# Gate and up products of two FFNs as seven block products instead of eight, on one Trainium2 core

## The chip, the cores and the metric

The kernel runs on one NeuronCore of a Trainium2 chip. The metric is the device time of one launch in microseconds. Three runs of the kernel before gave 1391.13 us as their median, between 1390.26 and 1394.65 us. Engines are named as in the profile: PE multiplies matrices, PEld is its weight load, DVE and ACT work elementwise, POOL works elementwise and issues transfers whose descriptors it writes itself, SP issues the other transfers.

## The reference

Two layers, each a token mixer (RWKV-7 in layer 0, a gated spatial unit in layer 1) followed by a dense SwiGLU FFN, all between two RMS norms with a residual. Only the FFN and the norm ahead of it matter here (512 tokens, 1024 features, 2816 hidden features, all float32):

```
h = x * rsqrt(mean(x*x) + 1e-6) * gain          # per token
h = (silu(h @ w_gate) * (h @ w_up)) @ w_down    # 1024 -> 2816 -> 1024
x = x + rmsnorm(h) * gain_post
```

## The kernel before

Every float32 matrix product is made of three products of a shorter float type: each operand is split into a high part (an ACT copy that rounds) and a low part (a DVE subtraction of the rounded from the raw), and `mm3` (line 153) adds high·high, high·low and low·high into one PSUM bank. `weight` (line 134) loads a 512 KB weight tile through SP's queue, casts it on ACT (line 131 or 147) and subtracts on DVE (line 132) or, for the first tiles of a stage, on POOL (line 148). Two buffers of raw weights and four of split ones let these run ahead of PE.

The order is RWKV, FFN 0, spatial unit, FFN 1. Each ends in `out_proj` (line 229), which multiplies by the output matrix in two column halves and keeps the last weight units for the end, so that the tokens finish in four blocks of 128: `post0` and `post1` make the norm behind the product and the new residual `x`, and the next stage's norm follows two blocks behind (`norm.step`). `Norm.step` (line 48) transposes the raw `x` on PE, multiplies by the gain and splits into `hT`; the factor 1/rms of each token is left out and comes in behind the products: `Norm.row` (line 70) spreads the four columns of factors over all partitions as a row `yb`.

In `ffn` (line 302) a loop goes over 22 tiles `j` of 128 hidden features. For each, the gate and the up weight tile (128 columns, all 1024 rows as 8 blocks `kt`) are multiplied by `hT`: 2 x 8 x 3 = 48 matmuls of 512 tokens; the first two tiles do it in two halves of 256 tokens, because the later tokens' norm comes later. Then line 330 (DVE) multiplies the gate result by `yb`, line 331 (ACT) applies silu, line 332 (DVE) multiplies by the up result, line 333 (POOL) by `yb`, and the product is split at once for the down product.

The program is written in one order; a planner with a cost model decides at compile time the order of each engine's instructions and gives out the buffers. PSUM has eight banks, given to stages by the tables `BANKS_RWKV` and `BANKS` (lines 28 to 30). SBUF has 17 slots of tag "s" and, in the stages behind RWKV, 13 of tag "x", each of 4 KB per partition.

Of the kernel before, what the change touches and what calls it, by code (L numbers as in the profile page):

```python
# [7 lines left out]
F32 = mybir.dt.float32  # L8
# [5 lines left out]
P = 128  # L14
# [15 lines left out]
BANKS = dict(pa=(3, 4, 0, 7), pb=(1, 2, 5, 6), h0=(1, 2, 5, 6), h1=(3, 4, 0, 7), tr=(1, 2, 5, 6))  # L30
# [9 lines left out]
class Norm:  # L40
# [29 lines left out]
    def row(self):  # L70

        k, nc = self.k, self.k.nc
        t = k.sm.tile([P, D], F32, name="hn", tag="hn", bufs=2)
        yb, dg = t[:, 0:T], t[:, T:2 * T]
        pt = k.bank("tr", "yb")
        for tt in range(TT):
            nc.gpsimd.tensor_scalar(dg[:, tt * P:(tt + 1) * P], k.ident, self.y[tt][:, 0:1], None, op0=ALU.mult)
        nc.tensor.matmul(pt, k.ones, dg, start=True, stop=True)
        nc.scalar.copy(yb, pt)
        return yb  # L80


class Trunk:
# [69 lines left out]
    def mm3(self, out, lhs, rhs, start, stop):  # L153

        mm = self.nc.tensor.matmul
        mm(out, lhs[0], rhs[0], start=start, stop=False)  # L156
        mm(out, lhs[0], rhs[1], start=False, stop=False)  # L157
        mm(out, lhs[1], rhs[0], start=False, stop=stop)  # L158
# [64 lines left out]

    def start_x(self, xts, norm):
        for tt in range(TT):
            norm.step(tt, xts[tt])
        norm.finish()
# [74 lines left out]
    def ffn(self, li, xts, norm, store=None, nxt=None):  # L302
        nc = self.nc
        gains = self.i["norm_gains"]
        wg = self.i["ffn_w_gate"][li].rearrange("(kt p) n -> p kt n", p=P)
        wu = self.i["ffn_w_up"][li].rearrange("(kt p) n -> p kt n", p=P)
        wd = self.i["ffn_w_down"][li].rearrange("(u j p) n -> u p j n", p=P, j=2)
        acts = []
        hT, yb = norm.hT, None
        def products(j, ws, acc, a, b):  # L310
            for w, ps in zip(ws, acc):
                for kt in range(KT):
                    self.mm3(ps[:, a:b], (w[0][:, kt, :], w[1][:, kt, :]), (hT[kt][:, 0, a:b], hT[kt][:, 1, a:b]),
                             kt == 0, kt == KT - 1)

        first = []
        for j in range(NJ):
            if not first:
                for n in range(j, j + 1):
                    cols = slice(n * P, (n + 1) * P)  # L320
                    first.append(([self.weight(w[:, :, cols], pool=n < 2) for w in (wg, wu)],
                                  [self.pa("gu") for _ in range(2)]))
                halves = ((0, 256), (256, 512)) if j < 2 else ((0, 512),)
                for a, b in halves:
                    for ws, acc in first:
                        products(j, ws, acc, a, b)
            pp = first.pop(0)[1]
            sg = self.fp.tile([P, T], F32, name="sg", tag="sg", bufs=1)
            yb = norm.row() if yb is None else yb
            nc.vector.tensor_tensor(sg, pp[0], yb, op=ALU.mult)  # L330
            nc.scalar.activation(sg, sg, AF.Silu)
            nc.vector.tensor_tensor(sg, sg, pp[1], op=ALU.mult)  # L332
            nc.gpsimd.tensor_tensor(sg, sg, yb, op=ALU.mult)  # L333
            act = self.slot([P, 2, T], F32R, "act", "x" if j < XSLOTS else "s")
            self.split(act[:, 0, :], act[:, 1, :], sg)
            acts.append(act)
        self.out_proj(lambda k: (acts[k][:, 0, :], acts[k][:, 1, :]), lambda u: wd[u], NJ, gains[li, 3], xts, store, norm=nxt)
# [33 lines left out]
    def rwkv(self, x0, nxt):  # L371
# [3 lines left out]
        with ExitStack() as ctx:  # L375
# [619 lines left out]
            norm = self.prenorm("g02") if nxt else None  # L995
# [4 lines left out]
    def sgu(self, xts, norm, nxt):  # L1000
# [64 lines left out]
        for m in range(8):  # L1065
# [3 lines left out]
            t = self.fp.tile([P, T], F32, name="sg", tag="sg", bufs=1)  # L1069
# [10 lines left out]
def build(tc, ins, out, only=None):  # L1080
    with ExitStack() as ctx:
# [6 lines left out]
        norm = None  # L1088
        if only in (None, "rwkv"):
            xts, norm = k.rwkv(xts, only is None)  # L1090
        if only != "rwkv":
            k.tags = BANKS
            k.fp = ctx.enter_context(tc.tile_pool(name="fp", bufs=1))
            k.wx = ctx.enter_context(tc.tile_pool(name="wx", bufs=2))
            k.sx = ctx.enter_context(tc.tile_pool(name="sx", bufs=1))

        def begin(col, norm):
            if norm is None:
                norm = k.prenorm(col)
                k.start_x(xts, norm)  # L1100
            return norm

        if only in (None, "ffn"):
            nxt = k.prenorm("g10") if only is None else None
            k.ffn(0, xts, begin("g02", norm), out[0] if only else None, nxt)
            norm = nxt
        if only in (None, "sgu"):
            nxt = k.prenorm("g12") if only is None else None
            k.sgu(xts, begin("g10", norm), nxt)
            norm = nxt  # L1110
        if only is None:
            k.ffn(1, xts, norm, out[0])
        elif only != "ffn":
            for t in range(TT):
                nc.sync.dma_start(out=out[0, t * P:(t + 1) * P, :], in_=xts[t])
# [26 lines left out]
```

## Time and profile before

| | |
|---|---|
| median of three runs | 1391.13 us |
| span of the profiled execution | 1389.8 us |
| PE busy in it | 1326.0 us (95%) |
| DVE / ACT / POOL busy | 753.5 / 604.0 / 224.9 us |
| FFN 0, first gate matmul to first down matmul | 483.3 to 735.9 us |
| FFN 1, first gate matmul to last | 1012.0 to 1260.4 us |
| bytes moved in the whole span | 139.90 MB, mean 101 GB/s |

The profile gives for the profiled execution only its span, so sums are made against 1389.8 us; the median of the runs lies 1.3 us above. Busy time of PE is modelled: a matmul of 512 columns is shown with 0.39 us, though the next starts 0.23 us after it. So the distance between starts is what is read in the following, not the duration. A span's busy share is a mean over stages; the FFN's gate and up stage is read by itself.

### The profile page before, as it was taken

To read this page: it belongs to the slowest core of one execution; us is meant where nothing else is said; L and a number is where in the kernel's file an instruction comes from. 1 tells how busy PE (TensorE), PEld (TensorE's weight loads), DVE (VectorE), ACT (ScalarE), POOL (GpSimd) and SP (SyncE) were. 2 spreads that over 40 slices of the span, in tenths; PEclk is the share of its full clock that TensorE was granted. 3 is DMA by queue.
4 is the path that set the end of the run, shared out by engine and by line. 5 is a ranking of instruction groups with operands and counts; after the bars stand their busy time and mean duration, and the time that the engine had idled before them with its cause. 6 is when DMAs were issued, how large, how long until landed. Compare 5 with 4: busy or idle time off the path is not lost.

```text
span 1389.8 us, 21566 instructions
## 1 busy us (share of the span) xinstructions
PE 1326.0 (95%) x8512; PEld 1080.3 (78%) x8512; DVE 753.5 (54%) x1309; ACT 604.0 (43%) x1100; POOL 224.9 (16%) x347
## 2 busy tenths in 40 slices
PE   5989999988899899999999999999999999999998
PEld 3657789877776698888888887878888888888886
DVE  7875666577746565455542325575565544453223
ACT  7865785667343453232322224542463322232121
POOL 1000283675000121111110002010221111110000
PEclk9999999999799999999999999999999999999999
DMA  5135594323114143333333232342323333322331
GB/s 154 44 97 145 139 223 153 101 75 94 67 46 148 48 120 94 103 92 91 91 91 106 92 106 91 106 137 76 91 83 98 93 91 98 100 91 91 92 105 61
DMA packets 216100, 139.90 MB, mean 101 GB/s; under 512 B 66704, under 2 KB 192192, under 8 KB 216000
## 3 DMA queue, kind: packets, MB, share of 16 engines
q1 hardware_dynamic: 214704, 133.81, 33.1%
q0 software_dynamic: 1296, 4.72, 1.0%
q8 instruction: 67, 1.10, 0.3%
q14 instruction: 33, 0.27, 0.1%
HBM read 124.35 MB, written 14.16 MB: 100 GB/s over the span
## 4 chain that ended last, share of the span: by engine, by line
PE 83%; DVE 6%; ACT 4%; DMA 3%; issue 2%; POOL 1%; SPq 0%; DVEq 0%; ACTq 0%; POOLq 0%
PE gu L156 12%; PE gu L158 12%; PE gu L157 12%; PE acc L156 9%; PE acc L157 8%; PE acc L158 8%; PE proj L157 2%; PE proj L156 2%; PE proj L158 2%; PE gh L821 2%; PE lora L494 1%; PE lm L706 1%; PE u L157 1%; PE u L158 1%; PE u L156 1%
## 5 line engine op out<-in xcount | busy, mean ns | idle before, releaser
L131 ACT CAST whi<-wraw 128x1024 fp32r<-128x1024 f32 x177 | 185.8, 1049 | 487.4 <-PE gu L157 252.6
L132 DVE TENSOR_TENSOR wlo<-wraw,whi 128x1024 fp32r<-128x1024 f32 x177 | 263.1, 1486 | 226.0 <-ACT whi L131 218.5
L157 PE MATMUL gu<-hT,whi 128*128 128x512 f32 (+1 forms) x768 | 288.6, 377 | 1.4 <-DVE hT L59 1.4
L156 PE MATMUL gu<-hT,whi 128*128 128x512 f32 (+1 forms) x768 | 289.1, 379 | 0.3 <-ACT hT L57 0.3
L158 PE MATMUL gu<-hT,wlo 128*128 128x512 f32 (+1 forms) x768 | 288.6, 377 | 0.0
L157 PEld LDWEIGHTS gu<-hT,whi 128*128 128x128 f32 x768 | 145.1, 189 | 30.5 <-DVE hT L59 1.6
L156 PEld LDWEIGHTS gu<-hT,whi 128*128 128x128 f32 x768 | 145.0, 190 | 29.4 <-ACT hT L57 0.5
L158 PEld LDWEIGHTS gu<-hT,wlo 128*128 128x128 f32 x768 | 144.9, 189 | 28.6
L157 PE MATMUL acc<-wlo,act 128*128 128x512 f32 x416 | 163.8, 394 | 0.0
L156 PE MATMUL acc<-whi,act 128*128 128x512 f32 x416 | 163.7, 395 | 0.0
L158 PE MATMUL acc<-whi,act 128*128 128x512 f32 x416 | 160.4, 394 | 0.0
L333 POOL TENSOR_TENSOR sg<-sg,hn 128x512 f32<-128x512 f32 x44 | 58.0, 1318 | 417.4 <-DVE sg L332 417.4
L332 DVE TENSOR_TENSOR sg<-sg,gu 128x512 f32<-128x512 f32 x44 | 30.3, 688 | 142.4 <-PE gu L158 140.2
L158 PEld LDWEIGHTS acc<-whi,act 128*128 128x128 f32 x416 | 78.1, 188 | 18.2
L156 PEld LDWEIGHTS acc<-whi,act 128*128 128x128 f32 x416 | 78.2, 188 | 18.0
L157 PEld LDWEIGHTS acc<-wlo,act 128*128 128x128 f32 x416 | 78.1, 188 | 18.0
L330 DVE TENSOR_TENSOR sg<-gu,hn 128x512 f32<-128x512 f32 x44 | 30.4, 691 | 67.3 <-PE gu L158 67.1
L131 ACT CAST act<-sg 128x512 fp32r<-128x512 f32 x52 | 32.4, 622 | 73.4 <-POOL sg L333 59.2
L156 PE MATMUL proj<-xsp,whi 128*128 128x512 f32 x128 | 52.2, 413 | 3.5 <-ACT xsp L131 3.1
L157 PE MATMUL proj<-xsp,whi 128*128 128x512 f32 x128 | 52.2, 409 | 2.2 <-DVE xsp L132 2.2
L148 POOL TENSOR_TENSOR wlo<-wraw,whi 128x1024 fp32r<-128x1024 f32 x12 | 29.0, 2424 | 145.4 <-ACT whi L147 145.4
L158 PE MATMUL proj<-xsp,wlo 128*128 128x512 f32 x128 | 52.1, 408 | 0.1
(321 smaller groups left out, 2187.5 us busy)
## 6 DMA issues: line engine op xcount, KB each, us to landing
wraw<-in_ffn_w_gate_dram SPq DMA_DIRECT2D x44, 512.0 KB
wraw<-in_ffn_w_up_dram SPq DMA_DIRECT2D x44, 512.0 KB, 3.8
wraw<-in_ffn_w_down_dram SPq DMA_DIRECT2D x44, 512.0 KB, 3.6
wraw<-in_rwkv_w_rkv_dram SPq DMA_DIRECT2D x24, 512.0 KB, 4.5
wraw<-in_sgu_w_in_dram SPq DMA_DIRECT2D x16, 512.0 KB, 3.7
x<-in_x_dram SPq DMA_DIRECT2D x8, 512.0 KB, 5.9
ST<-sb SPq DMA_DIRECT2D x8, 512.0 KB, 6.3
MV<-sa SPq DMA_DIRECT2D x32, 128.0 KB, 3.2
```

Of the source, the lines that this page charges most:

```text
L131: self.nc.scalar.copy(hi, src)
L132: self.nc.vector.tensor_tensor(lo, src, hi.bitcast(F32), op=ALU.subtract)
L148: nc.gpsimd.tensor_tensor(lo, raw, hi.bitcast(F32), op=ALU.subtract)
L156: mm(out, lhs[0], rhs[0], start=start, stop=False)
L157: mm(out, lhs[0], rhs[1], start=False, stop=False)
L158: mm(out, lhs[1], rhs[0], start=False, stop=stop)
L330: nc.vector.tensor_tensor(sg, pp[0], yb, op=ALU.mult)
L332: nc.vector.tensor_tensor(sg, sg, pp[1], op=ALU.mult)
L333: nc.gpsimd.tensor_tensor(sg, sg, yb, op=ALU.mult)
L494: mm(acc, w1m[j][:, kt].rearrange("p j n -> p (j n)"), src(kt), start=j == 0 and kt == 0, stop=j == 1 and kt == KT - 1)
L706: mm(lm[:, cc * P:(cc + 1) * P], st[:, cc].rearrange("p n t -> p (n t)"), mv[:, cc, :, hd, :], start=True, stop=True)
L821: mm(gh[:, cc * P:(cc + 1) * P], mt[rows, cc, :], bx[rows, 0:2, cc, :], start=True, stop=True)
```

## The change

The gate and up products of each FFN are done for two hidden tiles (a pair `n`, 11 pairs) at a time as 2 x 2 blocks: two halves of the contraction, two hidden tiles, two halves of the tokens. A plain block product takes eight products of a block; here it takes seven, of sums of blocks. A product is now 2 (gate, up) x 4 (kt) x 3 = 24 matmuls of 256 tokens with 24 weight blocks; its gate and up results share one PSUM bank, 256 columns each.

- The token side: `Mixed` takes the place of `Norm` ahead of the FFNs. It finishes the norm before the transpose (squares, root, one DVE multiplication of the whole 128 x 1024 block), so `yb` and line 333 are gone. Blocks 1 and 2 (the first 256 tokens) are split when the second token block is there; `combine` makes and splits the five others from sums once all four are there.
- The weight side: per pair three single blocks are loaded by SP (`quad`), and each of the seven operands is cast on ACT and subtracted on DVE. Four operands are sums. Two of them (`dsum`) are made by transfers on POOL's queue: one that writes, and one with `accum_op` that adds to what is there, each as two transfers of 256 KB for gate and up; the two others are DVE additions onto the first sum.
- The results: three banks R, Q, Z gather products, with partial sums copied by ACT from Q, R and Z; Q starts as a copy of R into PSUM, and matmuls go on adding to it, for which one matmul in each Q bank is issued first.
- The order in a pair is p5, p6, p7, p3, p4 for the first two pairs, whose p1 and p2 are done ahead of `combine`, and p1, p5, p6, p2, p7, p3, p4 afterwards.
- The split of the hidden activation for the down product moves into `out_proj`, where it is done when first used. POOL no longer subtracts the first weight tiles of an FFN.

```diff
-BANKS = dict(pa=(3, 4, 0, 7), pb=(1, 2, 5, 6), h0=(1, 2, 5, 6), h1=(3, 4, 0, 7), tr=(1, 2, 5, 6))
+BANKS_F0 = dict(tr=(1, 2), R=(3, 4), Q=(5, 0), Z=(7, 6), h0=(1, 2, 4, 0), h1=(3, 5, 7, 6))
+BANKS_SGU = dict(tr=(1, 2), pa=(3, 5, 7, 6), h0=(1, 2, 4, 0), h1=(3, 5, 7, 6))
+BANKS_F1 = dict(tr=(1, 2), R=(4, 0), Q=(3, 5), Z=(7, 6), h0=(1, 2, 0, 5), h1=(4, 3, 7, 6))
...
+class Mixed:
...
+    def split(self, name, src, tag):
+        k = self.k
+        hi, lo = (k.slot([P, 4, 256], F32R, "bc", tag) for _ in range(2))
+        k.split(hi, lo, src)
+        self.b[name] = (hi, lo)
+
+    def step(self, tt, xt):
...
+        t = k.sm.tile([P, D], F32, name="hn", tag="hn", bufs=2)
+        s = [k.sumsq(xt[:, c:c + 512], t[:, c:c + 512]) for c in (0, 512)]
+        y = k.rsqrt1(s[1], k.part(s[0], 1.0 / D, RMS_EPS), 1.0 / D)
+        v.scalar_tensor_tensor(t, xt, y[:, 0:1], self.gain, op0=ALU.mult, op1=ALU.mult)
+        for j in range(2):
+            pt = k.bank("tr", "ptr")
+            for n in range(4):
+                kt = 4 * j + n
+                nc.tensor.transpose(pt[:, n * P:(n + 1) * P], t[:, kt * P:(kt + 1) * P], k.ident)
+            nc.scalar.copy(self.raw[j, l][:, :, (tt % 2) * P:(tt % 2 + 1) * P], pt.rearrange("p (n t) -> p n t", n=4))
+        if tt == 1:
+            self.split(1, self.raw[0, 0], "s")
+            self.split(2, self.raw[1, 0], "s")
...
+    def combine(self):
+        k, v = self.k, self.k.nc.vector
+        b11, b21, b12, b22 = (self.raw[p] for p in ((0, 0), (1, 0), (0, 1), (1, 1)))
+        t1, t2 = (k.slot([P, 4, 256], F32, "tsum", "x") for _ in range(2))
+        v.tensor_tensor(t1, b11, b12, op=ALU.subtract)
+        self.split(5, t1, "x")
+        v.tensor_tensor(b12, b22, b12, op=ALU.subtract)
+        v.scalar_tensor_tensor(t2, b12, -1.0, b11, op0=ALU.mult, op1=ALU.subtract)
+        self.split(6, t2, "x")
+        self.split(7, b12, "x")
+        self.split(3, b22, "x")
+        v.scalar_tensor_tensor(b21, t2, -1.0, b21, op0=ALU.mult, op1=ALU.subtract)
+        self.split(4, b21, "x")
...
     def ffn(self, li, xts, norm, store=None, nxt=None):
...
+        def quad(n, j, f):
+            pool, tag = ((self.wp, "wraw"), (self.f0p, "f0"), (self.gp, "gain"))[loads[0] % 3]
...
+            for m, w in enumerate(wgu):
+                nc.sync.dma_start(out=t[:, m], in_=w[:, 4 * j:4 * j + 4, (2 * n + f) * P:(2 * n + f + 1) * P])
+            return t
+
+        def product(ps, name, src, start=False):
+            self.nw += 1
+            wp = self.wx if self.nw % 2 else self.wp
+            hi, lo = (wp.tile([P, 2, 4, P], F32R, name=t, tag=t, bufs=2) for t in ("whi", "wlo"))
+            self.split(hi, lo, src)
+            bh, bl = b[name]
+            for m in range(2):
+                for kt in range(4):
+                    self.mm3(ps[:, 256 * m:256 * m + 256], (hi[:, m, kt], lo[:, m, kt]), (bh[:, kt], bl[:, kt]),
+                             start and m == 0 and kt == 0, m == 1 and kt == 3, True)
+
+        def dsum(n, *parts):
+            s = self.slot([P, 2, 4, P], F32, "wsum", "x")
+            for op, (j, f) in zip((ALU.bypass, ALU.add), parts):
+                for m, w in enumerate(wgu):
+                    nc.gpsimd.dma_start(out=s[:, m], in_=w[:, 4 * j:4 * j + 4, (2 * n + f) * P:(2 * n + f + 1) * P], accum_op=op)
+            return s
+
+        def p1(n):
...
+            product(o["R"], 1, o["a11"], True)
...
+            a.copy(o["Q"], o["R"])
...
+        def p5(n):
...
+            o["a22"] = quad(n, 1, 1)
+            o["s"] = dsum(n, (0, 1), (1, 1))
...
+            product(o["Z"], 5, o["s"], True)
...
+            a.copy(o["t"][:, 0], o["Z"])
+
+        def p6(n):
+            o = pairs[n]
+            v.tensor_tensor(o["s"], o["s"], o["a11"], op=ALU.add)
+            product(o["Q"], 6, o["s"])
+            a.copy(o["t"][:, 1], o["Q"])
+
+        def p7(n):
+            o = pairs[n]
+            product(o["Q"], 7, dsum(n, (0, 0), (0, 1)))
...
+            v.scalar_tensor_tensor(o["cc"][:, 1], o["Q"], -1.0, o["t"][:, 0], op0=ALU.mult, op1=ALU.subtract)
+
+        def p3(n):
+            o = pairs[n]
+            v.tensor_tensor(o["s"], o["s"], o["a12"], op=ALU.add)
+            product(o["Z"], 3, o["s"])
+            cc = o["cc"]
+            v.tensor_tensor(cc[:, 0], o["Z"], o["t"][:, 1], op=ALU.add)
+            a.activation(cc[:, :, g], cc[:, :, g], AF.Silu)
+            v.tensor_tensor(o["act"][:, :, u], cc[:, :, g], cc[:, :, u], op=ALU.mult)
+
+        def p4(n):
+            o = pairs[n]
+            product(o["Q"], 4, o["a22"])
+            gate(o["act"][:, 1, g], o["Q"], -1.0)
+
+        for n in range(2):
+            p1(n)
+            p2(n)
+        norm.combine()
+        for n in range(NJ // 2):
+            for p in (p5, p6, p7, p3, p4) if n < 2 else (p1, p5, p6, p2, p7, p3, p4):
+                p(n)
+
+        halves = {}
+
+        def down(k):
+            if k not in halves:
+                t = halves[k] = self.slot([P, 2, T], F32R, "actw", "x" if k < XSLOTS else "s")
+                self.split(t[:, 0], t[:, 1], acts[k // 2][:, k % 2])
+            return halves[k][:, 0], halves[k][:, 1]
```

`p2(n)` loads the fourth kind of single block as p1 does, multiplies it by block 2 into R and applies `gate` (a silu of 256 columns on ACT and a DVE product with the up half).

More of the change, by code (lines that the diff above doesn't have):

```diff
@@ L303, in ffn @@
         nc = self.nc
+        v, a = nc.vector, nc.scalar
         gains = self.i["norm_gains"]
-        wg = self.i["ffn_w_gate"][li].rearrange("(kt p) n -> p kt n", p=P)
-        wu = self.i["ffn_w_up"][li].rearrange("(kt p) n -> p kt n", p=P)
+        wgu = [self.i[n][li].rearrange("(kt p) n -> p kt n", p=P) for n in ("ffn_w_gate", "ffn_w_up")]
         wd = self.i["ffn_w_down"][li].rearrange("(u j p) n -> u p j n", p=P, j=2)
[L308 to L336, printed above, removed]
@@ new lines, in dsum @@
+        def dsum(n, *parts):
[5 more added lines that the diff above has]
+        def p1(n):
+            o = pairs[n] = dict(act=self.slot([P, 2, T], F32, "act"))
+            acts.append(o["act"])
+            o["a11"] = quad(n, 0, 0)
+            o["R"] = self.bank("R", "R")
+            product(o["R"], 1, o["a11"], True)
+            if len(seeded) < 2:
+                q = self.bank("Q", "Q")
+                seeded.append(q)
+                bh = b[1][0]
+                nc.tensor.matmul(q, bh[:, 0, 0:P], bh[:, 0:2].rearrange("p k t -> p (k t)"), start=True, stop=True)
+            o["Q"] = seeded[n % 2]
+            a.copy(o["Q"], o["R"])
@@ new lines, in gate, with p2 @@
+        def gate(dst, src, sign=1.0):
+            sg = self.fp.tile([P, 256], F32, name="sg", tag="sg", bufs=2)
+            a.activation(sg, src[:, g], AF.Silu, scale=sign)
+            if sign == 1.0:
+                v.tensor_tensor(dst, sg, src[:, u], op=ALU.mult)
+            else:
+                v.scalar_tensor_tensor(dst, src[:, u], sign, sg, op0=ALU.mult, op1=ALU.mult)
+        def p2(n):
+            o = pairs[n]
+            o["a12"] = quad(n, 1, 0)
+            product(o["R"], 2, o["a12"])
+            gate(o["act"][:, 0, g], o["R"])
@@ new lines, in p4 @@
+        def p4(n):
+            o = pairs[n]
+            product(o["Q"], 4, o["a22"])
[13 more added lines that the diff above has]
+            return halves[k][:, 0], halves[k][:, 1]
@@ L340, in load_features @@
+        self.out_proj(down, lambda u: wd[u], NJ, gains[li, 3], xts, store, norm=nxt)
     def load_features(self):
```

84 lines of the change are left out of this document (44 added, 40 removed).

## The prediction

> **What bounds the kernel now.** I read the page's totals and chain first.
>
> ```profile
> span 1389.8 us, 21566 instructions
> PE 1326.0 (95%) x8512; PEld 1080.3 (78%) x8512; DVE 753.5 (54%) x1309; ACT 604.0 (43%) x1100; POOL 224.9 (16%) x347
> ...
> PE 83%; DVE 6%; ACT 4%; DMA 3%; issue 2%; POOL 1%; SPq 0%; DVEq 0%; ACTq 0%; POOLq 0%
> ```
>
> PE carries 83% of the chain that ended last. Next I read busy time by stretch for the two gate and up stages (columns: length, then PE, PEld, DVE, ACT, POOL busy with counts, granted clock, DMA share, GB/s).
>
> ```profile
> 484.00:510.00 26.00, 23.94 (x184) 23.25 (x185) 19.42 (x60) 17.41 (x49) 8.62 (x8) 0.93 0.34 98
> 510.00:735.00 225.00, 225.00 (x984) 182.48 (x983) 114.61 (x104) 69.20 (x84) 27.30 (x21) 1.00 0.34 98
> ...
> 1035.00:1260.00 225.00, 225.00 (x980) 182.08 (x980) 113.37 (x104) 68.64 (x83) 27.04 (x21) 1.00 0.33 98
> ```
>
> In both, PE never pauses, at full clock; DVE is half busy, ACT a third, the DMA engines a third. So these stages last as long as their matmuls, and fewer columns streamed means less time, as long as the others keep up. What a matmul costs is the distance of starts. In the timeline, line 332 runs once per hidden tile, at the same place of each; between two 256-column rows there are 18 matmuls.
>
> ```profile
> 602.38 0.69 DVE L332 TENSOR_TENSOR sg<-sg,gu 128x512 f32<-128x512 f32 x1 [3.55 <-PE gu L158]
> ...
> 635.82 0.69 DVE L332 TENSOR_TENSOR sg<-sg,gu 128x512 f32<-128x512 f32 x1 [3.55 <-PE gu L158]
> ```
> ```profile
> 502.38 0.28 PE L156 MATMUL gu<-hT,whi 128*128 128x256 f32 x1
> ...
> 504.52 0.28 PE L156 MATMUL gu<-hT,whi 128*128 128x256 f32 x1
> ```
>
> Three tiles of 48 matmuls take 33.44 us: 0.2322 us per 512 columns. 18 matmuls of 256 take 2.14 us: 0.119 us, or 2.4% more per column. That price already holds a new weight block for every matmul.
>
> **The change: PE.** A pair had 2 x 48 = 96 matmuls of 512: 22.29 us. It gets 7 x 24 = 168 of 256: 19.99 us, 2.30 us less, a product taking 2.86 us. Over 11 pairs that is 25.3 us; the first two tiles were in halves already (96 more of 256 each pair of halves: 192 x 0.119 = 22.85 against 22.29), another 0.6. Two FFNs: 2 x 25.9 = **-51.8 us**. The four matmuls that open the Q banks and the two dropped ones of `yb` cancel to half a microsecond.
>
> **The steady pair on the other engines.** These rows price what it needs (duration; or count, min/median/max in ns).
>
> ```profile
> L132 DVE TENSOR_TENSOR wlo<-wraw,whi x177: 1177/1226/2367, 19.1 to 1361.8; 128x1024 fp32r<-128x1024 f32 x177
> L132 DVE TENSOR_TENSOR act<-sg,act x52: 676/678/693, 516.4 to 1264.0; 128x512 fp32r<-128x512 f32 x52
> ```
> ```profile
> L131 ACT CAST act<-sg 128x512 fp32r<-128x512 f32 x52 | 32.4, 622 | 73.4 <-POOL sg L333 59.2
> ```
> ```profile
> L131 ACT CAST whi<-wraw 128x1024 fp32r<-128x1024 f32 x41 | 43.1, 1052 | 122.0 <-PE gu L157 119.4 <-DMA wraw<-in_ffn_w_up_dram 2.0 <-DMA wraw<-in_ffn_w_gate_dram 0.6
> L331 ACT ACTIVATE sg<-sg 128x512 f32<-128x512 f32 x22 | 13.9, 633 | 4.1 <-DVE sg L330 4.0
> ```
> ```profile
> 465.45 0.42 DVE L930 TENSOR_TENSOR ob<-gate,ob 128x256 f32<-128x256 f32 x1 [1.83 <-PE gate L929]
> 507.94 0.59 ACT L79 COPY hn<-yb 128x512 f32<-128x512 f32 x1
> 603.15 1.30 POOL L333 TENSOR_TENSOR sg<-sg,hn 128x512 f32<-128x512 f32 x1 [9.84 <-DVE sg L332]
> 603.17 2.37 DVE L132 TENSOR_TENSOR wlo<-wraw,whi 128x1024 fp32r<-128x1024 f32 x1
> ```
>
> DVE: seven subtractions and two additions of 1024 at 1.23 = 11.1 us, one combination of 512 from PSUM, one addition, one product (0.69 each) and two gates of 256 (0.42): 14.0 us of 20.0. ACT: seven casts at 1.05, three PSUM copies at 0.59, a silu of 0.63 and two of 256 (bounded by 0.63 each): 11.0 us. Neither binds. POOL's multiplication and DVE's subtraction, which started together (603.15 and 603.17), stretched the latter to 2.37; with line 333 gone that doubling goes, worth nothing now, but it is why 1.23 is the price afterwards.
>
> The waits inside a pair: ACT's copy of R into Q has p5 between it and the next user, the copy of Q after p6 has p2, DVE's read after p7 has p3, each a cover of 2.86 us for 0.6 to 0.7. So nothing, except in the first two pairs, where p2 follows p1 and p7 follows p6 directly; without the cover each costs about 0.9 us (0.59 and a handover). The split of the activations moves into the down stage: 0.62 + 0.68 us each, two per unit of 24 x 0.2322 = 5.57 us beside a weight's 1.05 and 1.23; ACT 2.3 and DVE 2.6 of 5.57, hidden.
>
> **The transfers.** SP issues six of 256 KB per pair instead of four of 512 KB. POOL issues eight, which no row shows in this size or with accumulation; the nearest:
>
> ```profile
> L1008 POOL DMA_DIRECT2D wsr<-in_sgu_ws_dram x1: 988/988/988, 800.2 to 800.2; - x1
> ...
> DMA to landing us min/median/max: 5.6/5.6/5.6
> ```
> ```profile
> L180 POOL DMA_DIRECT2D gain<-in_norm_gains_dram x4: 531/534/758, 408.4 to 979.5; - x4
> ```
>
> `wsr` has 1024 rows of 512 bytes, a gain 128 of 4 KB; 512 rows lie between, some 0.75 us of issue: 6 us per pair. Two halves of a plain `dsum` land within 5.6 us (twice the bytes). Bytes: 2.62 MB plain per pair, at the stage's 98 / 0.34 = 288 GB/s 9.1 us of the DMA engines, and 1.05 MB accumulated, from the same rate (3.6 us) to a third of it (10.9 us; it reads two places and writes one): 12.7 to 20.0 of 20.0 us. I take half the rate, 7.3: 82%, not binding. The chain of one sum is two issues, a landing, two issues, a second landing of X, cast and subtraction: 1.5 + 5.6 + 1.5 + X + 1.05 + 1.23 = 10.9 + X, and its buffer comes free only after the subtraction (of 13 "x" slots ten hold token blocks, three rotate). It is hidden to X = 9.1. I take X = 5.6, hidden, and keep the rest as a rival. Behind a waiting second transfer on POOL stand only the next sum's transfers; behind a cast that waits for them stand ACT's bank copies, and so PE.
>
> The Trainium skill (SBUF — State Buffer, "SBUF: two separate sides") says that a DVE operation in a 2-port mode keeps POOL from writing descriptors until it ends. No run here shows it; if each of the eight issues waited out one subtraction, POOL would need 8 x (0.75 + 1.23) = 15.8 us of 20, an estimate that leaves the sum alone.
>
> **The start of each FFN.** Here the change costs.
>
> ```profile
> 479.65 0.39 PE L158 MATMUL acc<-whi,oT 128*128 128x512 f32 x1
> ...
> 483.31 0.50 PE L156 MATMUL gu<-hT,whi 128*128 128x256 f32 x2 [0.27 <-ACT hT L57]
> ```
> ```profile
> L156 PE MATMUL acc<-whi,act x416: 387/393/484, 735.9 to 1382.1; 128*128 128x512 f32 x139
> ```
> ```profile
> 1006.69 0.40 PE L158 MATMUL acc<-whi,act 128*128 128x512 f32 x1
> ...
> 1011.97 1.20 PE L156 MATMUL gu<-hT,whi 128*128 128x256 f32 x4
> ```
> ```profile
> L158 PE MATMUL gu<-hT,wlo x768: 276/394/415, 485.8 to 1260.4; 128*128 128x512 f32 x160, 128*128 128x256 f32 x32
> ```
>
> Matmuls now need 20 x 11.15 + 22.85 = 245.8 us. From the end of the last residual product to the stage's end FFN 0 takes 735.9 - 479.9 = 256.0, FFN 1 1260.6 - 1006.9 = 253.7: 10.2 and 7.9 us lost. Afterwards DVE has a queue here. Large rows not yet shown:
>
> ```profile
> L270 DVE TENSOR_TENSOR hn<-acc,gain x16: 673/691/693, 468.7 to 1383.8; 128x512 f32<-128x512 f32 x16
> L1047 DVE SCALAR_TENSOR_TENSOR vt<-vt,lmu,gain x4: 1270/1277/1279, 912.5 to 916.7; 128x1024 f32<-128x1024 f32 x4
> ```
> ```profile
> 490.34 0.14 DVE L207 RECIPROCAL rr<-rr 128x1 f32<-128x1 f32 x1
> ...
> 490.52 0.22 DVE L208 SCALAR_TENSOR_TENSOR rt<-rr,rm 128x1 f32<-128x1 f32 x1
> ...
> 491.10 0.75 DVE L273 SCALAR_TENSOR_TENSOR x<-f,ry,x 128x512 f32<-128x512 f32 x1
> ```
>
> From the last residual product to the last subtraction of pair 0, DVE does: the last block's residual 0.69 + 2 x 0.75 + some 0.7 of single-column ones (four at 0.14 to 0.22) = 2.9; three `step`s of 1.28 + 1.0 (five or six of these) = 6.9; blocks 1 and 2, 2.5; two weight subtractions of the four early products (two fit into free buffers before), 2.5; two gates 0.8; `combine`'s four sums and five subtractions, 11.1; pair 0 without its last gate, 8.6 + 0.7 x 3 + 0.4 = 11.1. Sum 37.8 us; p4 then ends 2.9 later, 40.7. PE's nine products need 25.7. So 15.0 lost, which holds the wait for the norm (5.1 in FFN 1 today), and the early copies lie in it. Pair 1's copy adds 0.9, and the half clock after a pause (0.93 over 26 us above, 1.8 us) once more: 17.7. That is 7.5 and 9.8 over today: **+17.3 us**. Bounds: no more than today, 0; DVE idle a quarter of the time while it waits for ACT, 12.6 more per FFN: +42.5.
>
> **Sum.** 1389.8 - 51.8 + 17.3 = 1355.3 on the profiled execution, with its 1.3 us to the median **1357 us**. Own range: 1339 to 1382.
>
> **Rivals.**
> 1. *The start costs nothing more* (19%). Eleven microseconds of early products, needing only half the tokens, cover the norm, where today 5.7 do, and ACT copies whole banks instead of eight pieces. Against: the DVE sum above. 1391.1 - 51.8 = 1339.
> 2. *The sums come late* (15%). The slot of a sum turns round in 10.9 + X. From X = 9.1 it sets the pair; each microsecond more costs 20 us (ten pairs per FFN behind the first). At X = 10.8 the gain is gone; at twice `wsr`'s landing, 11.2, the time is 1357 + 20 x 2.1 = 1399, slower. For: the second landing must follow the first, and the DMA engines may be over 82% full. Against: POOL's plain transfers land in 5.6 with twice the bytes. The Trainium skill (DMA: Bandwidth & Descriptors, "Rules for kernel authors") has an accumulating transfer read its destination and write it later, so the wait between the two cannot go; it gives no price.
> 3. *Columns are not what PE pays for* (4%): with 3696 instead of 2304 weight loads, a matmul of 256 would have to cost 22.29 / 168 = 0.133 us for no gain, 1391 + 17 = 1408. Against: 0.119 over stretches of new weights each time; for: those last only some ten microseconds.
>
> **How the numbers follow.** The forecast has 62%. This kernel's runs differ by 0.3% (4.2 us), so "same" is 1387 to 1395. Faster: the forecast, rival 1 and a fifth of rival 2 (0.84); same: a fifth of rival 2 (0.03); slower: the rest of 2, and 3 (0.13). The range takes rival 1 in, and of rival 2 what lies below 1390: 1335 to 1390.
>
> **What would show it.** PE's starts 0.119 us apart in the middle of the FFNs and 20.0 us per pair: right on PE. Pauses of PE in the first 45 us of each FFN released by DVE, some 18 us in all: right on the start. Casts of `wsum` or DVE's additions to it waiting for a transfer in the steady pairs, a landing of the accumulating transfers over 9 us: rival 2. Wrong altogether: a pair over 22 us, or PE busy throughout with starts over 0.13 us apart.

## The result and the profile after

The changed kernel takes 1403.35 us as the median (1398.48 to 1405.32), the kernel before on the same chip 1391.13 us: a ratio of 1.0088, with an interval of 1.0059 to 1.0117. (One run of 2500.06 us, far off all others, is left out; so is one of 3142.71 us of an experiment.) It is slower by 12 us where I predicted 34 us less. The profiled execution, the fastest of the runs, has a span of 1396.5 us, 6.7 more than before; the stretches below account for these 6.7.

From the page of the changed kernel: the totals, the busy times and the chain that ended last.

```profile
span 1396.5 us, 24884 instructions
PE 1281.8 (92%) x9904; PEld 1122.3 (80%) x9904; DVE 854.0 (61%) x1415; ACT 703.0 (50%) x1218; POOL 325.2 (23%) x465
...
PE 77%; DVE 7%; ACT 6%; DMA 6%; issue 2%; POOL 1%; SPq 0%; DVEq 0%; ACTq 0%; POOLq 0%
```

PE is busy 44 us less, and its share of the chain fell from 83% to 77%: the time went to DVE, ACT and the transfers. Where, the stretches tell (columns as in the prediction). First the kernel before at the start of each FFN, then the kernel after at the starts and in the middle of the FFNs.

```profile
470.00:530.00 60.00, 54.52 (x334) 48.03 (x334) 41.91 (x106) 33.70 (x84) 16.43 (x12) 0.97 0.33 94
1012.00:1060.00 48.00, 48.00 (x302) 43.17 (x301) 27.38 (x70) 23.92 (x55) 6.64 (x8) 0.98 0.30 88
```
```profile
470.00:530.00 60.00, 31.29 (x184) 28.41 (x183) 40.57 (x75) 29.58 (x57) 13.60 (x14) 0.75 0.46 96
530.00:740.00 210.00, 209.18 (x1739) 208.09 (x1738) 145.05 (x158) 110.25 (x149) 78.12 (x77) 1.00 0.84 176
1012.00:1060.00 48.00, 23.43 (x151) 22.15 (x152) 32.33 (x52) 24.02 (x44) 12.39 (x12) 0.72 0.50 100
```

In the middle PE still hardly pauses. At the starts it fell from 54.5 to 31.3 us busy out of 60 and from 48.0 to 23.4 out of 48. The pair itself came out as predicted; the row of DVE's combination after p7, four pairs apart:

```profile
612.68 0.69 DVE L438 SCALAR_TENSOR_TENSOR cc<-Q,hn 128x512 f32<-128x512 f32 x1 [1.52 <-PE Q L213]
...
692.64 0.69 DVE L438 SCALAR_TENSOR_TENSOR cc<-Q,hn 128x512 f32<-128x512 f32 x1 [1.52 <-PE Q L213]
```

79.96 us for four pairs: 19.99 each. To see what a whole gate and up stage costs, I take the rows of PE that bound it, in FFN 0: the last residual product, the first down matmul, and the last product of the last pair, which now stands among the down matmuls.

```profile
476.88 0.40 PE L213 MATMUL acc<-whi,oT 128*128 128x512 f32 x1
...
734.00 0.40 PE L213 MATMUL acc<-whi,actw 128*128 128x512 f32 x1
...
739.01 0.40 PE L213 MATMUL Q<-bc,whi 128*128 128x256 f32 x2
...
741.83 0.40 PE L213 MATMUL acc<-wlo,actw 128*128 128x512 f32 x1
```

From 477.11 (a start later) to 734.00, and 2.82 for that last product: 259.7 us. The 77 products need 11 x 19.99 = 219.9, so 39.8 us are lost; in FFN 1, by the same rows, 38.8. Before it was 10.2 and 7.9. So the matmuls gave back 51.8 us and the starts took 29.6 + 30.9 = 60.5, where I had put 17.3. That makes +8.7; the span grew by 6.7. The 2.0 between lie outside these bounds, mostly ahead of FFN 0, whose last residual product now starts at 476.88 instead of 479.65; part of that is transposes that used to stand among the residual products.

Where the 39.8 lie in FFN 0, in four stretches of the kernel after: to the first early product, to the end of the four early products, to product 5 of pair 0, and the first ten microseconds behind.

```profile
477.12:495.27 18.15, 2.98 (x18) 2.37 (x16) 13.74 (x38) 12.85 (x31) 0.00 (x0) 0.65 0.24 70
495.27:513.20 17.93, 16.00 (x114) 15.41 (x114) 11.69 (x17) 8.13 (x13) 1.49 (x2) 0.88 0.14 36
513.20:524.37 11.17, 0.04 (x1) 0.00 (x0) 4.95 (x7) 4.25 (x5) 9.32 (x8) 0.65 0.93 166
524.37:534.26 9.89, 8.83 (x50) 8.34 (x50) 8.47 (x7) 5.34 (x6) 3.02 (x4) 0.70 1.10 223
```

18.1 us pass with nothing but transposes on PE; the four early products, 11.4 us at full speed, take 17.9; 11.2 us pass before product 5; the last 4 are a granted clock near one half (0.70 over the last stretch) and small waits behind that. PE's rows that end the pauses:

```profile
487.77 1.94 PE L116 MATMUL ptr<-ident,hn 128*128 128x128 f32 x8 [9.62 <-DVE ry L267]
495.27 0.58 PE L213 MATMUL R<-bc,whi 128*128 128x256 f32 x1 [5.55 <-ACT bc L188]
...
524.37 0.79 PE L213 MATMUL Z<-bc,whi 128*128 128x256 f32 x2 [11.14 <-ACT whi L188]
```

The last one is the pause that I had not foreseen at all: product 5 waits for the cast of its weight sum. ACT's and POOL's rows in the timeline say why it is late.

```profile
523.28 1.04 ACT L188 CAST whi<-wsum 128x1024 fp32r<-128x1024 f32 x1 [6.80 <-DMA wsum<-in_ffn_w_up_dram]
```
```profile
474.39 0.77 POOL L388 DMA_DIRECT2D wsum<-in_ffn_w_gate_dram  x1 [58.58 <-DVE ry L267]
...
511.16 0.75 POOL L388 DMA_DIRECT2D wsum<-in_ffn_w_gate_dram  x1 [35.24 <-DVE bc L189]
...
514.68 0.75 POOL L388 DMA_DIRECT2D wsum<-in_ffn_w_gate_dram  x1 [2.04 <-DVE bc L189]
```

POOL issued the first transfers of the first sum at 474. The next instructions on its queue are the first transfers of the second sum (511.16) and of the third (514.68), and these wait for buffers that DVE's splits in `combine` free. The adding transfers of the first sum stand behind both and went out from 516 on: a sum that could have been there near 485 (an estimate: the adding transfers 4 us behind the first ones, and 6 us to land) came at 523.

### The profile page after: what moved, and what is told of

Read it like the earlier page. It is cut to its first block, busy times and chain, and to the rows that moved or that the text cites. A ratio compares the mean times of both kernels' runs of the same rounds, so it can differ in the third digit from the quotient of the medians.

```text
span 1396.5 us, 24884 instructions
## 1 busy us (share of the span) xinstructions
PE 1281.8 (92%) x9904; PEld 1122.3 (80%) x9904; DVE 854.0 (61%) x1415; ACT 703.0 (50%) x1218; POOL 325.2 (23%) x465
## 4 chain that ended last, share of the span: by engine, by line
PE 77%; DVE 7%; ACT 6%; DMA 6%; issue 2%; POOL 1%; SPq 0%; DVEq 0%; ACTq 0%; POOLq 0%
PE acc L213 26%; PE Q L213 13%; PE Z L213 9%; PE R L213 8%; PE proj L213 5%; PE u L213 3%; PE v L213 3%; PE gh L954 2%; DMA wsum<-in_ffn_w_up_dram 2%; PE lm L839 1%; PE mp L947 1%; ACT whi L188 1%; PE Yp L996 1%; ACT hn L246 1%; DMA wq<-in_ffn_w_up_dram 1%
## 5 line engine op out<-in xcount | busy, mean ns | idle before, releaser
L189 DVE TENSOR_TENSOR wlo<-wraw,whi 128x1024 fp32r<-128x1024 f32 x97 | 119.1, 1228 | 186.7 <-ACT whi L188 182.9
L213 PE MATMUL acc<-whi,actw 128*128 128x512 f32 x704 | 220.5, 394 | 0.0
L213 PE MATMUL Q<-bc,whi 128*128 128x256 f32 x1056 | 191.0, 281 | 2.2 <-DVE cc L438 2.2
L213 PEld LDWEIGHTS Q<-bc,whi 128*128 128x128 f32 x1056 | 162.9, 189 | 2.5 <-DVE cc L438 2.4
L213 PEld LDWEIGHTS acc<-whi,actw 128*128 128x128 f32 x704 | 132.3, 188 | 30.4
L213 PE MATMUL Z<-bc,whi 128*128 128x256 f32 x704 | 135.2, 288 | 22.5 <-ACT whi L188 22.5
L213 PE MATMUL Q<-bc,wlo 128*128 128x256 f32 x528 | 148.5, 281 | 0.0
L213 PE MATMUL R<-bc,whi 128*128 128x256 f32 x704 | 134.0, 285 | 14.0 <-ACT bc L188 10.1
L213 PE MATMUL acc<-wlo,actw 128*128 128x512 f32 x352 | 138.5, 394 | 0.0
L388 POOL DMA_DIRECT2D wsum<-in_ffn_w_up_dram x88 | 121.4, 1450 | 2.3 <-DMA wsum<-in_ffn_w_up_dram 2.3
```

Source lines behind the costliest of these rows:

```text
L189: self.nc.vector.tensor_tensor(lo, src, hi.bitcast(F32), op=ALU.subtract)
L213: self.nc.tensor.matmul(out, l, r, start=start, stop=stop, skip_group_check=resumed)
L388: nc.gpsimd.dma_start(out=s[:, m], in_=w[:, 4 * j:4 * j + 4, (2 * n + f) * P:(2 * n + f + 1) * P], accum_op=op)
```

## The experiments

Two theories. **A, order**: each engine works in the order written for it, and at an FFN's start the rows that PE needs next stand behind others: the first sum's adding transfers behind later sums, the norm of the first two token blocks behind the residuals of the later ones, the cast of the first sum behind all of `combine`. **B, amount**: the work that the change adds to the start, the sums and splits of `combine` above all, is too much for DVE and ACT before pair 0, in whatever order. The runs go from the order to the amount. "Lost" is the figure of 39.8 us worked out above, for FFN 0 of each run's profile; it differs by 2 us between two profiles of one kernel (the third experiment).

The experiments ran on other chips, where the kernel before takes 1386 to 1388 us, and the changed kernel was not run there. So what counts is the ratio to the kernel before, 1.0088 for the changed kernel; a time is compared with an expected range only loosely.

### POOL's order

```diff
-                    nc.gpsimd.dma_start(out=s[:, m], in_=w[:, 4 * j:4 * j + 4, (2 * n + f) * P:(2 * n + f + 1) * P], accum_op=op)
+                    with (self.tc.issue_after(last[-1]) if last and n < 3 else nullcontext()):
+                        ins = nc.gpsimd.dma_start(out=s[:, m], in_=w[:, 4 * j:4 * j + 4, (2 * n + f) * P:(2 * n + f + 1) * P], accum_op=op)
+            last.append(ins.ins)
```

The first pairs' sums are transferred one after the other on POOL's queue.

> Only the order on POOL's queue is changed: in each FFN the adding transfers of the first three pairs' sums are issued ahead of the next sum's first transfers. Theory A (the sum of p5 of pair 0 comes late because its second transfer stands behind two other sums' first transfers, which wait for a buffer until DVE has split blocks 5 and 6): the pauses of 11.1 and 10.6 us ahead of the first Z product go, part of it comes back as a wait of 3 to 6 us for the sum of p7, and the whole is 8 to 16 us faster than the changed kernel: 1387 to 1395 us. Theory B (the prediction's: DVE's queue of sums and subtractions holds PE there): DVE is finished at 518 in either case, the pause keeps to within 3 us of what it is, 1399 to 1403 us.

Measured: 1396.01 us, ratio to before 1.0046 (1.002 to 1.0072); lost 37.3 us.

```profile
513.55 0.80 PE L213 MATMUL Z<-bc,whi 128*128 128x256 f32 x2 [4.24 <-ACT whi L188]
```

The pause ahead of product 5 fell from 11.14 to 4.24 us (FFN 1: from 10.55 to 5.19), the others stayed. So POOL's order held that product up, for 5 to 7 us. Some of it came back at pair 1, whose sums are now later: 2.23 us ahead of its product 5. By the ratios the time fell by 0.4%, some 6 us, less than theory A's 8 to 16 and more than theory B's 0 to 4.

### The norm one block behind instead of two

```diff
+        lag = 1 if isinstance(norm, Mixed) else LAG
...
-            if norm and tt >= LAG:
-                norm.step(tt - LAG, xts[tt - LAG])
+            if norm and tt >= lag:
+                norm.step(tt - lag, xts[tt - lag])
```

> Only the norm's step ahead of the FFNs follows one token block behind the residual product instead of two. Theory A (the first early product starts 18.2 us after the last residual product because the second block's squares, root and scaling stand on ACT and DVE behind the third and fourth block's work): the first product starts some 8 to 12 us sooner, but the sum's queue on POOL still decides pair 0, which follows the fourth block: 3 to 5 us per FFN, 1393 to 1398 us. Rival (the chain of the norm itself is that long): the start moves by under 3 us, 1400 to 1405 us.

Measured: 1393.55 us, 1.0039 (1.001 to 1.0068); lost 36.6 us.

```profile
482.15 0.58 PE L213 MATMUL R<-bc,whi 128*128 128x256 f32 x1 [3.42 <-ACT bc L188]
...
514.53 0.80 PE L213 MATMUL Z<-bc,whi 128*128 128x256 f32 x2 [15.06 <-ACT whi L188]
```

The time is in theory A's range. The early products begin 11.2 us after the last residual product instead of 18.2, but the pause ahead of product 5 grows from 11.1 to 15.1: over half of what one wait gave, the next took.

### Both, and the weight buffers in another pattern

The two edits above, and the single weight blocks take the three kinds of buffers in another order:

```diff
-            pool, tag = ((self.wp, "wraw"), (self.f0p, "f0"), (self.gp, "gain"))[loads[0] % 3]
+            pool, tag = ((self.wp, "wraw"), (self.f0p, "f0"), (self.gp, "gain"))[(0, 1, 0, 2, 1, 2)[loads[0] % 6]]
```

> Both of the above, and the first four single blocks take other buffers (the one that waits for the gain row comes fourth instead of third, so that ACT's cast no longer waits for it). Theory A: the pauses ahead of the first early product and ahead of the first Z product both shrink, together 10 to 16 us per FFN: 1371 to 1385 us. Theory B: what is won ahead of the early products is lost again waiting for DVE ahead of pair 0: 1392 to 1400 us.

> The kernel with the norm one block behind, POOL's order and the new pattern of the weight buffers, once more, for its size against the kernel before and beside the two with pieces: 0.995 to 1.001 of before.

Measured: 1385.42 us, 0.9983 (0.9951 to 1.0014), and on another chip 1391.34 us, 1.0019 (1.0001 to 1.0036): within 0.2% of the kernel before. The second lies just above the 0.995 to 1.001 expected of it. By the ratios that is 10 to 15 us less than the changed kernel, where theory A had 18 to 32 and theory B 3 to 11. Lost 32.5 and 34.6 us. ACT's and PE's rows of the first:

```profile
508.75 2.93 ACT L188 CAST bc<-braw 128x1024 fp32r<-128x1024 f32 x3
511.58 1.04 ACT L188 CAST whi<-wsum 128x1024 fp32r<-128x1024 f32 x1
```
```profile
512.68 0.80 PE L213 MATMUL Z<-bc,whi 128*128 128x256 f32 x2 [9.96 <-ACT whi L188]
```

The sum lands in time now, and its cast stands behind the five casts of `combine`.

A variant, with two of the first sums in other buffers so that they need not wait for `combine`:

```diff
-            s = self.slot([P, 2, 4, P], F32, "wsum", "x")
+            s = self.slot([P, 2, 4, P], F32, "wsum", "s" if len(last) in (1, 2) else "x")
```

> As the one before, and the second and third sum (p7 of pair 0, p5 of pair 1) lie in buffers of the other tag, which are free at that time, so that they need not wait for combine's. Theory A: another 2 to 5 us per FFN, 1364 to 1380 us, and no wait for a sum over 2 us is left. Theory B: no different from the kernel before it.

Measured: 1391.29 us, 1.0018 (0.9994 to 1.0042), the same pause of 9.96 us: theory B of this run. Those buffers were not what was left.

### The blocks of `combine` one at a time

In the kernel of the last section, `combine` yields behind each block's split and so gives its blocks one by one: the one for product 5 first, each next one queued on ACT and DVE behind the split of the product before it.

```diff
-        norm.combine()
+        pieces = norm.combine()
...
+                if n == 0:
+                    first = p is p5
+                    with (nullcontext() if first else self.tc.issue_after(self.pcut[0])), \
+                         (nullcontext() if first else self.tc.issue_after(self.pcut[1])):
+                        next(pieces)
                 p(n)
```

> The kernel with the norm one block behind, POOL's order and the new pattern of the weight buffers, and in it the five blocks of combine as pieces: the block for product 5 first, and each next one (6, 7, 3, 4) queued on ScalarE and VectorE behind the casts and subtractions of the product before it. The amount of work on every engine is that of the kernel without the pieces. Theory A (order in the queues, not amount of work): the cast of the first sum no longer stands behind five casts; the pause ahead of the first Z falls from 9.96 us to 2 to 5 us in both FFNs, small pauses of 1 to 2 us come ahead of the next products, and the time falls from 1385 to 1373 to 1380 us, below the kernel before. Theory B (the amount of VectorE and ScalarE work in the start decides): the same time is lost in pauses ahead of products 6, 7, 3 and 4 instead, and the time stays within 1383 to 1388 us.

Measured: 1391.88 us, 1.005 (1.0023 to 1.0076), lost 35.9 us. The pause fell as theory A says; the time didn't. PE's rows, then three stretches of two microseconds:

```profile
504.28 0.89 PE L218 MATMUL Z<-bc,whi 128*128 128x256 f32 x2 [3.52 <-ACT whi L193]
...
516.09 0.51 PE L218 MATMUL Q<-bc,whi 128*128 128x256 f32 x2 [1.62 <-ACT whi L193]
...
540.07 0.50 PE L218 MATMUL Z<-bc,whi 128*128 128x256 f32 x2 [3.51 <-ACT whi L193]
```
```profile
512.00:514.00 2.00, 2.00 (x19) 2.00 (x18) 2.00 (x3) 1.05 (x1) 0.00 (x0) 1.00 0.08 23
514.00:516.00 2.00, 0.47 (x4) 0.26 (x3) 2.00 (x2) 1.50 (x3) 0.82 (x2) 1.00 0.81 239
516.00:518.00 2.00, 1.47 (x6) 1.25 (x7) 1.95 (x3) 2.00 (x4) 0.72 (x1) 0.74 0.61 174
518.00:520.00 2.00, 2.00 (x11) 2.00 (x11) 2.00 (x3) 0.87 (x1) 1.06 (x2) 0.50 0.28 92
```

DVE is busy nearly all the time from 504 to 520, as in the first, second and fourth of these stretches, and PE waits a little ahead of most products of pairs 0 and 1: 12.6 us in pauses from there on, against 14.0 in the kernel without pieces. But the pauses are scattered, and four stretches at a granted clock of 0.50 follow instead of one. The time is above both theories' ranges, and theory A's 1373 to 1380 us is clearly out. That is not yet proof of theory B: the pauses of pair 1 (0.95, 0.76 and 3.51 us) come when DVE is mostly idle (1.67 us of 6.00 in 522 to 528), and of the waits of ACT's casts behind them the longest, 3.62 us, is for the transfer of a weight sum.

With only the first block ahead and the other four in one go:

```diff
+                if n == 0 and p is p5:
+                    next(pieces)
+                if n == 0 and p is p6:
+                    with self.tc.issue_after(self.pcut[0]), self.tc.issue_after(self.pcut[1]):
+                        for _ in pieces:
+                            pass
```

> As the kernel with the pieces, but only the block for product 5 goes ahead of the first sum's split; the other four blocks follow it at once, so that they are done, and the sums' buffers free, earlier than with one piece ahead of each product. Theory A: the pause ahead of the first Z stays at about 3.5 us, pair 1's first product no longer waits for its sum (1.0 and 3.5 us and half-clock stretches with the pieces), and the time is 1376 to 1383 us. Theory B (VectorE's amount of work): VectorE has 19 operations of 1.22 us between the last block's transposes and product 3's split, 23 us, and TensorE gets pauses of 9 us in all and half-clock stretches behind them wherever the work is put; the time stays at 1383 to 1392 us.

Measured: 1387.98 us, 1.0001 (0.9978 to 1.0024), lost 32.3 us: within theory B's range, 5 us above theory A's. PE's pauses from product 5 on are 10.1 us here, 4 less than without the pieces, and the loss is the same, since three stretches at a granted clock of 0.50 follow them.

Then three of the splits' subtractions on POOL, the sum for product 7 queued ahead of them (only the first part of the code is shown):

```diff
+        if name in (7, 3, 4):
+            k.nc.scalar.copy(hi, src)
+            k.nc.gpsimd.tensor_tensor(lo, src, hi.bitcast(F32), op=ALU.subtract)
...
```

> As the one before, with the subtractions of the splits of blocks 7, 3 and 4 on GpSimd (three operations; a subtraction of this size takes 2.42 us there in the kernel before), and the transfers for product 7's sum queued ahead of them. Theory B: it takes 3 of VectorE's 1.22 us operations, 3.7 us in each FFN, off the stretch that VectorE bounds, and shortens the time by 5 to 9 us against the one before, to 1374 to 1385 us. Theory A (order alone): no more than 2 us between the two.

Measured: 1404.16 us, 1.0127 (1.0091 to 1.0163), lost 42.8 us: neither theory. DVE's rows while POOL subtracts, and POOL's group:

```profile
514.82 1.22 DVE L455 TENSOR_TENSOR wsum<-wsum,wq 128x1024 f32<-128x1024 f32 x1
515.95 3.37 DVE L198 TENSOR_TENSOR bc<-tsum,bc 128x1024 fp32r<-128x1024 f32 x1
519.25 3.39 DVE L198 TENSOR_TENSOR wlo<-wq,whi 128x1024 fp32r<-128x1024 f32 x1
522.57 3.39 DVE L198 TENSOR_TENSOR wlo<-wsum,whi 128x1024 fp32r<-128x1024 f32 x1
```
```profile
L98 POOL TENSOR_TENSOR bc<-braw,bc 128x1024 fp32r<-128x1024 f32 x3 | 9.2, 3074 | 26.5 <-ACT bc L97 26.5
```

The three operations taken from DVE made three others of it last 3.4 us instead of 1.22, and took 3.07 each on POOL. The run says nothing on the theories; it says that here POOL could not take work off DVE.

### Without the adding transfers

This kernel leaves out the second term of the two weight sums that transfers make.

```diff
-            for op, (j, f) in zip((ALU.bypass, ALU.add), parts):
+            for op, (j, f) in zip((ALU.bypass,), parts):
```

> The changed kernel without the adding transfers: leaves out the second term of the two weight sums that transfers make, so 1.05 MB less moves per pair. Theory A (the adding transfers are hidden in the steady pairs and only hold up the first sum of an FFN through POOL's order): a pair stays at 20.0 us, the pause ahead of the first Z falls from 11.1 us to about 4 us as when POOL's order was changed, and the time is about that run's, 1390 to 1397 us. The DMA engines' share in 530 to 740 us falls from 0.84 to about 0.46, if the plain transfers take the 9.1 us a pair that I took and the adding ones the 7.8 us that are left. Theory C (the transfers hold up the steady pairs too): the pair gets shorter than 20.0 us and the time falls by 20 us or more.

Measured: 1385.62 us, 0.9994 (0.9973 to 1.0014), lost 32.5 us. The pause ahead of product 5 is 4.24 us and a pair stays at 19.99 us: theory A, and rival 2 of the prediction is out for the steady pairs. The time is some 4 us below theory A's range, and 0.5% below the run with POOL's order: the pauses that run had in pair 1 (2.23 and 0.76 us ahead of its product 5) are gone here, so the adding transfers hold up the start a little beyond the first sum.

```profile
517.53 0.80 PE L213 MATMUL Z<-bc,whi 128*128 128x256 f32 x2 [4.24 <-ACT whi L188]
```
```profile
530.00:740.00 210.00, 210.00 (x1729) 208.12 (x1728) 146.88 (x164) 111.00 (x152) 26.36 (x36) 1.00 0.42 123
```

The DMA engines' share falls from 0.84 to 0.42, the traffic from 176 to 123 GB/s: by this difference the adding transfers, 30% of the bytes, take half of the DMA engines' time.

### Without the work of `combine`

Products 5, 6, 7, 3 and 4 take blocks 1 and 2 in place of their own; the four sums and five splits are left out. In the changed kernel:

```diff
     def combine(self):
+        for name, same in ((5, 1), (6, 2), (7, 1), (3, 2), (4, 1)):
+            self.b[name] = self.b[same]
...
```

> The changed kernel without the work of combine: the five sums of activation blocks and their splits are left out, and the products 5, 6, 7, 3 and 4 take blocks 1 and 2 in their place. It takes 9 operations of 1.22 us from VectorE and 5 casts of 1.0 us from ScalarE in each FFN, and the buffers that made POOL's transfers wait for VectorE are free, so that POOL's order no longer holds up the first sum. Theory A (order in the queues): of the 41 us lost in the first FFN's start, the pause ahead of the first Z goes, 10 to 12 us in each FFN, and the pauses ahead of the first early product and inside the early products stay: 1373 to 1383 us. Theory B (VectorE's and ScalarE's amount of work is what the start costs): the pauses ahead of the early products shrink as well, and the time comes to 1357 to 1368 us, near the 1357 us that I predicted.

Measured: 1377.47 us, 0.9946 (0.9928 to 0.9964), lost 26.5 us: inside theory A's range. The pause ahead of product 5 is gone. That ahead of the first product grew from 5.55 to 10.86 us, so the run does not decide between the theories: with ten buffers free POOL issued sums for several pairs at once (busy 18.48 of 19.00 us ahead of the early products), and on the busy DMA engines ACT waited 9.53 us for a weight block of the early products.

```profile
476.00:495.00 19.00, 1.94 (x8) 1.57 (x8) 11.34 (x28) 8.39 (x22) 18.48 (x20) 0.56 1.12 254
```
```profile
492.26 1.04 ACT L178 CAST whi<-wq 128x1024 fp32r<-128x1024 f32 x1 [9.53 <-DMA wq<-in_ffn_w_up_dram]
```

So the same in the kernel with the better order, with the ten buffers held to the end of the FFN's gate and up stage:

```diff
+        self.held = [k.slot([P, 4, 256], F32, "bc", "x") for _ in range(10)]
+        for t in self.held:
+            v.tensor_copy(t[:, 0, 0:1], k.ones[:, 0:1])
...
```

> The kernel with the norm one block behind, POOL's order and the new pattern of the weight buffers, without the work of combine: the five sums of activation blocks and their splits are left out, products 5, 6, 7, 3 and 4 take blocks 1 and 2 in their place, and the ten buffers of the five blocks are taken all the same until the last pair, so that the sums' transfers run at the same distance ahead as before. If the work of combine between the early products and pair 0 is what is left of the loss once the order is better, the pause ahead of the first Z (9.96 us), the four short ones behind it (3.7 us) and the half clock after them (3 us) go in each FFN, 2 x 16.7 = 33 us: 1354 to 1362 us, beside 1385 to 1391 us with that work, and near the 1357 us that I predicted. If pair 0 is held up by its own weight sums and splits as well, pauses of 1 to 4 us stay ahead of its products, and the time is 1366 to 1376 us.

Measured: 1350.73 us, 0.9731 (0.97 to 0.9762), lost 16.8 us, 37 us faster than before and 4 us below the range expected. Here products 5 and on no longer wait for tokens 256 to 511 either, since blocks 1 and 2 are of the first 256: product 5 starts at 498.88, among the early products.

```profile
490.29 0.58 PE L213 MATMUL R<-bc,whi 128*128 128x256 f32 x1 [1.99 <-ACT bc L188]
...
498.88 0.48 PE L213 MATMUL Z<-bc,whi 128*128 128x256 f32 x2
```

So two things went at once, and the last run parts them: products 5, 7 and 4 take one unsummed block of the later tokens, 6 and 3 the other, with two splits and no sums.

```diff
-        for name, same in ((5, 1), (6, 2), (7, 1), (3, 2), (4, 1)):
+        self.split(5, self.raw[0, 1], "x")
+        self.split(6, self.raw[1, 1], "x")
+        for name, same in ((7, 5), (3, 6), (4, 5)):
```

> As the one before, but products 5, 7 and 4 take the block of the first rows of tokens 256 to 511, and 6 and 3 that of the other rows: two splits, no sums. The later products thus wait for the last token blocks again, as they do with combine; left out are four sums, three subtractions and three casts. If it was the work of combine that was taken away in the run before, the time is near that run's: the pause ahead of the first Z is 9.96 less four sums and three subtractions or so, 2 to 3 us, and the time 1355 to 1364 us. If most of it was that the later products no longer waited for tokens 256 to 511, the pause is 5 to 8 us with the half clock behind it, and the time 1368 to 1382 us.

Measured: 1365.5 us, 0.9835 (0.9799 to 0.9871), lost 23.8 us.

```profile
509.63 0.80 PE L215 MATMUL Z<-bc,whi 128*128 128x256 f32 x2 [3.56 <-ACT whi L190]
```

It fell between the two ranges expected: both count. Four sums, three subtractions and three casts cost 0.9983 - 0.9835 to 1.0019 - 0.9835 of the time, 1.5% to 1.8% or 21 to 26 us, 10 to 13 us in each FFN, though the seven DVE operations last only 7 x 1.22 = 8.5. Waiting for the later tokens and their two splits costs another 0.9835 - 0.9731, 1.0% or 14 us. The losses in FFN 0 say the same: 32.5 and 34.6 us with all of it, 23.8 here, 16.8 without either.

None of the versions with the whole computation beats the kernel before; the best of them equal it.

## Why the prediction was wrong

**PE: right.** 168 matmuls of 256 in 19.99 us per pair, as forecast. The 51.8 us came, and were spent again; without the work of `combine` and the wait for its tokens 37 of them reach the time.

**Steady pair: right.** Above, DVE is busy 145.05 of 210, 13.8 us per pair against 14.0 worked out; ACT 10.5 against 11.0. Little of it reaches PE, which is busy 209.18 of the 210.

**Transfers: right, and hidden.** A sum's transfers land in a median of 5.8 us (I took 5.6), the DMA engines are 84% busy (82%), the accumulated megabyte takes 0.42 x 20 = 8.4 us by the difference to the run without it (7.3). An 84% share leaves little room, but the pair stays at 19.99 us.

**Behind POOL's wait: wrong.** The sentence "Behind a waiting second transfer on POOL stand only the next sum's transfers" looked at the steady pair. At the start it is the other way round: the first sum's second transfers stand behind the first ones of later sums, and these wait for DVE. Undoing that order gave 5 to 7 us of the pause back in each FFN, and 0.4% of the time.

**The start: wrong, and this decided.** The step "From the last residual product to the last subtraction of pair 0, DVE does" 37.8 us, "so 15.0 lost". The work is right in sum, if not in every item (four early weight subtractions fall into the stretch, not two). From the timeline, the last subtraction of pair 0 begins at 533.04 and ends at 534.26:

```profile
477.12:534.26 57.14, 27.84 (x181) 26.11 (x179) 38.85 (x65) 30.56 (x54) 13.82 (x14) 0.73 0.49 105
```
```profile
DVE wlo L189 <- ACT whi L188: 9.3, 5, 6.2
DVE tsum L129 <- ACT braw L117: 5.9, 1, 5.9
```
```profile
501.00:507.00 6.00, 6.00 (x54) 6.00 (x54) 0.48 (x1) 2.64 (x6) 0.00 (x0) 1.00 0.31 90
```

DVE did 38.85 us of work in it, but in 57.14 us. I had let it run through as one queue. These 57.14 instead of 37.8 are 19.3 us, most of the 22.1 by which the 39.8 lost exceed the 17.7 that I had forecast. DVE idles 18.3 us, a third of the stretch, in turns with ACT, PE and POOL: it waits for ACT's casts ahead of its weight subtractions (9.3 us, of which 6.2 for that of the first sum, itself waiting for a transfer), and 5.9 us for the copy of the last block's transposes. In the first of these long waits PE idles too. In the second it doesn't: it runs the early products (6.00 of 6.00 above), and the last transposes stand among them, at 501.78 and 505.26, though DVE had finished their inputs by 500.65. So part of that wait may lie in PE's own order; no run changes it, and what it is worth stays open. My upper bound had "DVE idle a quarter of the time", +42.5 us for both FFNs; it was a third, and +60.5.

The runs show that none of the orders tried is the whole of it. Each change of order moves a pause and gives 2 to 8 us of 39.8; at best 32.3 are still lost. Without the work of `combine` and its wait for the later tokens 16.8 are; that this is near the 17.7 which I had forecast with them is chance. So order and amount both bear it: of the 39.8 us in FFN 0, 5 to 7 went with the better order; in that order four sums, three subtractions and three casts of `combine` are 9 to 11, and the wait for the later tokens with their two splits is 7. The chances I gave were too sure for the term that I had bounded most loosely. Rival 1, that the start costs nothing more, was the furthest from what happened. Rival 2's 1399 us and rival 3's 1408 lie near the 1403 measured by luck: a pair stayed at 19.99 us and 256 columns at 0.119, so neither was the mechanism. The one sum that came late was the first of each FFN, through POOL's order.

## What to carry to other kernels

A product that saves multiplications by sums of its operands can pay for the sums and splits where a stage begins, before its pipeline is full: sum up there not the work of the busiest engine but the chain of hand-overs between engines; here a third of the stretch was idle time. Ask of each queue, DMA issues included, what stands ahead of the first thing that the next engine needs when a buffer is not yet free. A saving per pair (here 2.3 us) needs enough pairs behind one start: at 11 pairs it was 25.9 us against a start of some 30.

## What the runs showed of the hardware

**POOL beside DVE.** A DVE subtraction of 128 x 1024 took 1.22 us alone and 3.37 to 3.39 while POOL did the same operation, and POOL's took 3.07 instead of the 2.42 of the kernel before. The Trainium skill (SBUF — State Buffer, "Who interferes with whom") says that a DVE instruction with two inputs in SBUF contends with a POOL instruction that reads SBUF, and that the loser blocks; the trace agrees: the three stretched operations lost 6.5 us together, more than the 3.7 us of the three that were moved.

**Short pauses and the clock.** In the run with the pieces the granted clock fell to 0.50 after a single pause of 3.5 us, but also after one of 1.62 us with one of 0.44 behind it (0.74, then 0.50 in the stretches shown), and after two of 0.95 and 0.76 us close together; it stayed there for 3 to 6 us. Single pauses of 1.30 us (the same kernel without the pieces), 1.93 us (the changed kernel) and even 2.92 us (the last run but one) were followed by a granted clock of 1.00, one of 2.85 us (the repeat of the better order) by 0.50. So the length of a pause alone does not tell. The Trainium skill (TensorE: Matmul & The Clock Gate, "Why this matters for your kernels") advises to have no idle gaps over about 3 us; here gaps of half that length cost the clock when they came close together. Spreading one pause of 10 us over several places thus gained nothing: with the first block ahead the pauses were 4 us shorter in all and the loss the same, and with all five pieces there were four stretches at 0.50 where there had been one.

**Accumulating transfers.** By the difference of the two DMA shares, 1.05 MB of accumulating transfers per pair took 8.4 us of the DMA engines' time, 125 GB/s, where the 2.62 MB of plain ones took 8.4 as well, 312 GB/s. One transfer of a sum landed in 5.8 us in the median with the second transfers among them and in 3.7 without.
